# One dependence graph for two instruction streams, list-scheduled per engine, in place of weaving two in-order lists

## Chip, cores, metric

One Trainium2 chip, eight cores, each with its own four sequences (data parallel; no traffic between cores). The metric is the device time in microseconds of the slowest core. Cores 0 to 3 are one die, 4 to 7 the other. In many executions of every kernel here (the one before showed clocks of 0.793 to 0.932 in the seven runs beside e1, five of them slow) the cores of one or both dies run at a lower granted TensorE clock; such a run is called slow, and is not compared with a fast one.

## The reference, cut to what matters

```python
# x (32, 2048, 1024) float32; two layers, each with three sub-layers; RMS norm after the last
for l in range(2):
    h = modulate(rms_norm(x, norm_ffn1[l]), sh1, sc1)
    x = x + 0.5 * g1 * swiglu(h, ffn1_w_gu[l], ffn1_w_down[l])        # d_ff 2816
    h = modulate(rms_norm(x, norm_mix[l]), sh2, sc2)
    x = x + g2 * token_mix(h, ...)   # one input projection; mixer A: dense attention, 6 heads;
                                     # B: windowed attention, 6 heads; C: latent attention, 4 heads;
                                     # gates, one output projection
    h = modulate(rms_norm(x, norm_ffn2[l]), sh3, sc3)
    x = x + 0.5 * g3 * swiglu(h, ffn2_w_gu[l], ffn2_w_down[l])
return rms_norm(x, final_norm)
```

## The kernel before

The whole program is written out as straight-line instructions, in tiles of 512 tokens. The builder first records two lists of operations. Stream F has the norms, feed-forward layers and projections, stream M the attention, gates and output projection. M of one sequence runs beside F of another. Each stream has its own buffers; in PSUM, F has two banks and M six. In the profiles fb is a bank of F, sb and ob are banks of M (scores and outputs above all), hF is F's normalised input, tmpf and nr are its scratch, q, kA, kB and kC are queries and keys by mixer, pT is the probabilities, mt is M's scratch; wF and wM are weights. QK is the product of queries and keys, PV that of probabilities and values. `weave` then merges the lists by a model of the chip, and the merged order becomes each engine's queue. Semaphore waits follow from recorded reads and writes.

```python
LAT = 0.1; MODE_SWITCH = 0.12; DMA_LAT = 2.0
DMA_RATE = 200e3        # bytes per us, one server for all queues
SLACK = 0.5

def weave(streams):
    # o.v = phase + share of the phase's TensorE work that lies before the operation
    ...
    while True:
        cands = []
        for i, st in enumerate(streams):
            if heads[i] >= len(st.ops):
                continue
            o = st.ops[heads[i]]                 # only the head of each stream
            if any(n not in toks for n in o.need):
                continue
            cands.append((est(o), i, o))         # modelled start
        ...
        mn = min(c[0] for c in cands)
        best = min((c for c in cands if c[0] <= mn + SLACK), key=lambda c: (c[2].v, c[0]))
        st = streams[best[1]]
        while True:                              # run the head, and what is glued to it
            o = st.ops[heads[best[1]]]; heads[best[1]] += 1
            run(o)                               # advances the engine, reads, writes; appends to order
            if not o.glue: break
    return order, max(et.values()), busy
```

The norm (F's statistics are eight matmuls with a matrix of ones):

```python
def rsqrt_rows(st, bk, br, nr, inv_n):           # all on VectorE, each depends on the one before
    ts(st, ms, bk[0:nr, :], inv_n, EPS, ALU.mult, ALU.add, [br], [nr_r[0]])
    ts(st, y.bitcast(I32), ms.bitcast(I32), -0.5, MAGIC, ALU.mult, ALU.add, [nr_r[0]], [nr_r[1]], fast=True)
    for _ in range(2):
        stt(st, t, y, -0.5, y, ALU.mult, ALU.mult, [nr_r[1]], [nr_r[2]])
        tt_(st, "dve", t, t, ms, ALU.mult, [nr_r[2], nr_r[0]], [nr_r[2]])
        stt(st, y, t, 1.5, y, ALU.add, ALU.mult, [nr_r[2], nr_r[1]], [nr_r[1]])

def norm(l, m, s):
    norm_stats()
    for c in range(KC):
        t, tr = tmp()
        tt_(F, "dve", t[:], xc(c), nr_y[:], ALU.mult, [xF_r[c], nr_r[1]], [tr])
        act(F, hc(c), t[:], AF.Identity, [tr, mods_r[l][m]], [hF_r[c]], scale=mA(l, m, s, c), bias=mB(l, m, s, c))
```

The softmax here doesn't subtract the row's maximum and nothing guards it: scores larger than these inputs give would overflow.

## Time and profile before

| | before |
|---|---|
| median of the first 3 runs (lowest to highest) | 17,184 us (16,484 to 17,991) |
| span of the profiled fast run, core 7 (core 0) | 16,515.5 (16,465.9) us |
| TensorE busy, core 7 | 14,310 us, 87% |
| mean granted clock, core 7 (core 0) | 0.929 (0.931) |
| core 0: TensorE idle / at half clock / of that, busy | 2,179 / 2,260 / 1,319 us |

Two of these three runs are slow ones, so the median says little; 16,484 is fast. The last row is from the trace's clock record and the matmuls in it. "Busy" counts matmuls at whatever clock they ran: on core 0 one of 512 columns follows another after 216 ns at full clock and after 427 ns at half (medians of start to start in this trace). A span therefore has three parts: idle time, half of the busy time that lay in half clock (lost to the clock), and the rest, which is the work at full clock and whatever else the profile counts as busy (drains, the tail of a matmul before a gap: an estimate, from the 0.38 us that a lone matmul shows against 0.216 in a row).

### The profile page before, as it was taken

What the parts mean: (1) busy time and instruction counts of PE and PEld (TensorE: products, weight loads), DVE (VectorE), ACT (ScalarE), POOL (GpSimd) and SP (SyncE); (2) the same over time, 40 slices, a digit from 0 to 9 for tenths busy, and PEclk for the clock granted to TensorE, in tenths of its full rate; (3) what the DMA queues carried; (4) which work ended last, traced back from release to release, by engine and by line L of the source; (5) the groups of instructions that cost most, each with busy time, mean ns of one, the idle gap of its engine ahead of it and who ended that gap; (6) DMA issues with size and microseconds to landing.
All of it is one profiled execution on the core that took longest, in us unless ns stands there. A gap on an engine that the chain in (4) does not pass through costs nothing.

```text
span 16515.5 us, 199324 instructions; the slowest of 8 cores (16449.4 to 16515.5 us)
## 1 busy us (share of the span) xinstructions
PE 14310.3 (87%) x63128; PEld 5831.8 (35%) x63128; DVE 6429.4 (39%) x8558; ACT 5883.1 (36%) x7980; POOL 1591.9 (10%) x1365
## 2 busy tenths in 40 slices
PE   7878887888898898899888998898898889888888
PEld 2323333333333333333333333333333333333333
DVE  2334333433434334434434434434433444434333
ACT  1123443332332433434414343234433333434421
POOL 0001111110001100101100010000001110010000
PEclk8989998999999999999999999999999999999988
DMA  8555435654446343545544444444445443344344
GB/s 215 166 178 148 130 112 155 147 151 143 130 151 174 126 128 119 158 134 164 143 149 142 134 156 136 146 123 128 135 137 153 139 140 117 125 145 132 107 135 133
DMA packets 949560, 2346.30 MB, mean 142 GB/s; under 512 B 221478, under 2 KB 332972, under 8 KB 940364
## 3 DMA queue, kind: packets, MB, share of 16 engines
q1 hardware_dynamic: 918604, 2235.36, 42.9%
q0 software_dynamic: 29952, 98.19, 3.9%
q8 instruction: 553, 9.06, 0.2%
q14 instruction: 451, 3.69, 0.1%
HBM read 2056.36 MB, written 375.00 MB: 147 GB/s over the span
## 4 chain that ended last, share of the span: by engine, by line
PE 74%; DVE 9%; issue 6%; ACT 6%; DMA 3%; POOL 1%; SPq 1%; DVEq 0%; ACTq 0%; POOLq 0%
PE fb L510 53%; PE sb L510 12%; PE ob L510 9%; ACT pT L519 3%; DVE nr L526 2%; DVE pT L522 1%; DVE tmpf L522 1%; ACT hF L519 1%; DVE mt L1121 1%; DVE nr L522 1%; ACT mt L519 1%; DVE nr L533 1%; DMA mt<-xs 1%; SPq L543 1%; POOL tmpf L522 1%
## 5 line engine op out<-in xcount | busy, mean ns | idle before, releaser
L510 PE MATMUL fb<-hF,wF 128*128 128x512 bf16 x25600 | 6927.5, 393 | 799.2 <-ACT hF L519 428.0
L510 PEld LDWEIGHTS fb<-hF,wF 128*128 128x128 bf16 x25600 | 2478.2, 100 | 4395.3 <-issue 1877.2
L510 PE MATMUL fb<-actb,wF 128*128 128x512 bf16 x11520 | 3042.3, 383 | 50.2 <-DMA wF<-wts 17.3
L519 ACT ACTIVATE pT<-sb 128x1024 bf16<-128x1024 f32 x2560 | 2514.8, 1024 | 1293.3 <-PE sb L510 1278.9
L510 PE MATMUL ob<-pT,vv 128*128 128x512 bf16 x6176 | 1855.0, 372 | 468.0 <-DVE pT L522 211.2
L519 ACT ACTIVATE tmpf<-fb 128x512 f32<-128x512 f32 (+1 forms) x1409 | 842.8, 598 | 3421.2 <-PE fb L510 3407.9
L526 DVE SCALAR_TENSOR_TENSOR tmpf<-tmpf,fb 128x512 f32<-128x512 f32 x1408 | 965.8, 686 | 2727.2 <-ACT tmpf L519 2598.0
L510 PEld LDWEIGHTS fb<-actb,wF 128*128 128x128 bf16 x11520 | 1117.7, 98 | 1485.1 <-issue 210.1
L522 DVE TENSOR_TENSOR actb<-tmpf,fb 128x512 bf16<-128x512 f32 x1536 | 1056.1, 688 | 1258.8 <-PE fb L510 1034.9
L510 PE MATMUL sb<-hM,wM 128*128 128x512 bf16 x4160 | 1297.1, 388 | 30.1 <-DMA wM<-wts_bf 30.1
L526 DVE SCALAR_TENSOR_TENSOR xF<-fb,modG,xF 128x512 f32<-128x512 f32 x512 | 384.4, 751 | 2339.9 <-PE fb L510 2338.6
L519 ACT ACTIVATE hF<-xF 128x512 bf16<-128x512 f32 x896 | 532.9, 627 | 1996.3 <-DVE xF L526 1493.0
L519 ACT ACTIVATE mt<-sb 128x512 f32<-128x512 f32 (+2 forms) x808 | 595.0, 737 | 1387.1 <-PE sb L510 1123.0
L522 POOL TENSOR_TENSOR o<-mt 128x512 bf16<-128x512 f32 x256 | 369.9, 1445 | 7385.7 <-DVE mt L1121 6686.3
L510 PEld LDWEIGHTS ob<-pT,vv 128*128 128x128 bf16 x6176 | 553.2, 99 | 1292.4 <-issue 834.5
L1121 DVE RECIPROCAL mt<-mt 128x512 f32<-128x512 f32 x256 | 857.9, 3351 | 46.2 <-ACT mt L519 34.6
L519 ACT ACTIVATE hF<-tmpf,mods,modA 128x512 bf16<-128x512 f32 x768 | 558.0, 805 | 871.8 <-DVE tmpf L522 871.6
L510 PE MATMUL sb<-q,kA 64*128 64x512 bf16 x3072 | 559.7, 394 | 330.3 <-ACT pT L519 175.2
L519 ACT ACTIVATE mt<-ob 64x512 f32<-64x512 f32 (+1 forms) x760 | 451.4, 594 | 698.0 <-PE ob L510 588.4
L510 PE MATMUL sb<-q,kC 96*128 96x512 bf16 x2048 | 698.7, 381 | 0.4 <-ACT pT L519 0.3
L522 POOL TENSOR_TENSOR mt<-mt 128x512 f32<-128x512 f32 x256 | 324.4, 1267 | 3658.3 <-DVE mt L526 3409.5
L540 DVE COPY mt<-ob 64x512 f32<-64x512 f32 x512 | 351.7, 687 | 821.7 <-PE ob L510 751.5
(77 smaller groups left out, 8862.1 us busy)
## 6 DMA issues: line engine op xcount, KB each, us to landing
wF<-wts_bf SPq DMA_DIRECT2D x1530, 512.0 KB, 3.8
wF<-wts_bf SPq DMA_DIRECT2D x960, 352.0 KB, 3.2
wM<-wts_bf SPq DMA_DIRECT2D x600, 512.0 KB, 4.3
wF<-adaw SPq DMA_DIRECT2D x144, 512.0 KB, 5.2
xs<-xF SPq DMA_DIRECT2D x128, 512.0 KB, 3.5
mt<-xs SPq DMA_DIRECT2D x256, 256.0 KB, 6.1
xs<-mt SPq DMA_DIRECT2D x256, 256.0 KB, 3.1
xF<-xs SPq DMA_DIRECT2D x128, 512.0 KB, 7.5
```

The costliest lines, as they stand in the source:

```text
L510: st.op("pe", lambda E: E.matmul(out, lhsT=lhsT, rhs=rhs, start=start, stop=stop, skip_group_check=True), reads=reads, writes=writes, cost ...
L519: st.op("act", lambda E: E.activation(out=out, in_=in_, func=func, **kw), reads=reads, writes=writes, cost=c_act(n))
L522: st.op(eng, lambda E: E.tensor_tensor(out=out, in0=a, in1=b, op=op), reads=reads, writes=writes, cost=c_dve(n) if eng == "dve" else c_poo ...
L526: st.op("dve", lambda E: E.scalar_tensor_tensor(out=out, in0=a, scalar=scalar, in1=b, op0=op0, op1=op1), reads=reads, writes=writes, cost= ...
L533: f = lambda E: E.tensor_scalar(out=out, in0=a, scalar1=s1, scalar2=s2, op0=op0, op1=op1)
L540: st.op("dve", lambda E: E.tensor_copy(out=out, in_=in_), reads=reads, writes=writes, cost=c_dve(n))
L543: st.op(eng, lambda E: E.dma_start(out=out, in_=in_), reads=reads, writes=writes, chan=chan, nbytes=nbytes, need=need, give=give)
L1121: M.op("dve", lambda E: E.reciprocal(out=den, in_=den), reads=[denr], writes=[denr], cost=c_rec(TT))
```

## The change

The intent is that an operation should not have to stand behind earlier operations of its own stream with which it shares neither data nor engine. The core of the diff:

```diff
-DMA_RATE = 200e3
-SLACK = 0.5
+DMA_RATE = 350e3
+CAST_SLOWER = 2.0
+SLACK = 0.25
+def dependences(streams):
+    ...                                   # o.ins: each predecessor through a read, write or queue
 def weave(streams):
-    heads = [0] * len(streams)
-    ...                                   # the loop shown above
+    dependences(streams)
+    fut = {e: [] for e in engs}           # per engine: known ready time, by time
+    av = {e: [] for e in engs}            # per engine: ready now, by o.v
+    while len(order) < n:
+        best = None
+        for e in engs:                    # the engine that can start something first
+            if av[e]: t = et[e]
+            elif fut[e]: t = max(et[e], fut[e][0][0])
+            else: continue
+            if best is None or t < best[0]: best = (t, e)
+        t, e = best
+        f, a = fut[e], av[e]
+        while f and f[0][0] <= t + SLACK:
+            r, q, o = heapq.heappop(f)
+            heapq.heappush(a, (o.v, q, o))
+        v, q, o = heapq.heappop(a)        # of those ready within SLACK, the oldest by phase
+        t = max(t, o.ready)
+        ...                               # advance the engine, release the successors
```

Cuts: glued operations become one unit with several instructions; the tokens `need` and `give` (a whole tile stored before another stream may load it) are replaced by reads and writes of each piece in DRAM; loads that cast from float32 count double in the model. No instruction, buffer or bank rotation changes.

## The prediction

> **What bounds the kernel now.** I read the page first, then the waits of TensorE, the windows by stage, and the timeline around single stalls. The page says that TensorE is the bound, not at its peak, and not at its full clock:
>
> ```profile
> PE 14310.3 (87%) x63128; PEld 5831.8 (35%) x63128; DVE 6429.4 (39%) x8558; ACT 5883.1 (36%) x7980; POOL 1591.9 (10%) x1365
> ...
> PEclk8989998999999999999999999999999999999988
> ...
> PE 74%; DVE 9%; issue 6%; ACT 6%; DMA 3%; POOL 1%; SPq 1%; DVEq 0%; ACTq 0%; POOLq 0%
> ```
>
> No other engine is busy for even 40% of the span, the DMA engines move 142 GB/s, and the chain that ended last lies on TensorE for 74%. The other 26% of it are hops through VectorE and ScalarE.
>
> The windows by stage (busy time by engine, granted clock, DMA share) show three stages. Up to 1,280 us and from 15,880 us on only the F stream (feed-forward layers, norms, projections) has work; between them F and the M stream (attention, gates) run together:
>
> ```profile
> 0.00:1280.00 1280.00, 1018.80 (x3799) 351.06 (x3800) 368.23 (x599) 270.42 (x406) 86.39 (x102) 0.90 0.64 180
> 1280.00:15880.00 14600.00, 12781.14 (x57155) 5272.12 (x57153) 5832.69 (x7623) 5498.41 (x7391) 1505.46 (x1263) 0.93 0.46 139
> 15880.00:16515.00 635.00, 510.36 (x2176) 208.59 (x2176) 228.51 (x336) 114.28 (x184) 0.00 (x0) 0.88 0.41 133
> ```
>
> The middle stage holds 1,819 of the 2,205 us in which TensorE is idle, though there two independent streams could cover for each other. The waits of TensorE in it say where (us in total, times, longest):
>
> ```profile
> PE fb L510 <- ACT hF L519: 443.9, 129, 24.7
> PE ob L510 <- DVE pT L522: 211.2, 101, 5.6
> PE sb L510 <- ACT pT L519: 158.4, 332, 10.1
> PE fb L510 <- DVE tmpf L522: 148.9, 64, 9.7
> ...
> PE sb L510 <- DVE mt L526: 119.9, 28, 24.2
> PE ob L510 <- DVE mt L540: 100.5, 119, 3.5
> ```
>
> The first and fourth are the norms: the first matmuls after a norm wait for hF. The others are attention: PV waits for the probabilities, QK for the exponential that frees its bank. One stall from the timeline (start, length, what, idle before it):
>
> ```profile
> 5954.03 0.69 DVE L533 TENSOR_SCALAR nr<-fb 128x512 f32<-128x512 f32 x1
> ...
> 5960.15 4.91 DVE L522 TENSOR_TENSOR tmpf<-xF,nr 128x512 f32<-128x512 f32 x8
> 5960.94 5.77 ACT L519 ACTIVATE hF<-tmpf,mods,modA 128x512 bf16<-128x512 f32 x8 [8.53 <-DVE tmpf L522]
> ...
> 5961.90 4.12 PE L510 MATMUL fb<-hF,wF 128*128 128x512 bf16 x6 [9.21 <-ACT hF L519]
> ```
>
> From the statistics to the first normalised chunk lie eight dependent VectorE operations, a multiply and an activation, some 8 us, and TensorE has nothing of M in its queue to do meanwhile. The clock pays too:
>
> ```profile
> 5940.00:5952.00 12.00, 11.17 (x56) 4.62 (x54) 4.02 (x6) 7.16 (x9) 0.00 (x0) 1.00 0.40 136
> 5952.69:5961.90 9.21, 0.01 (x2) 0.04 (x1) 8.23 (x13) 0.96 (x2) 0.00 (x0) 0.68 0.00 0
> 5961.90:5975.00 13.10, 9.71 (x37) 3.07 (x37) 11.49 (x14) 9.61 (x13) 1.78 (x1) 0.70 0.11 40
> ```
>
> The clock is 1.00 before the stall, and 0.68 and 0.70 in it and after it. In the trace's clock record core 7 spends 2,277 us at one half and 157 us at 0.8125.
>
> **The ledger of the span.** A dense stretch of F, 176 matmuls in 38.16 us, gives 216 ns for one 512-column matmul. 57,600 such slots (two 64-row matmuls that run side by side count as one) make 12,442 us, the fp32 ones 248, the narrower ones 284, and the 1,056 groups of 64-row matmuls add about 190 ns each at their borders (312 ns start to start instead of 216 in the trace), 200 us. So the work takes **13,170 us** at full clock and the span is 3,345 us above it. Of these 2,205 are idle. About 1,300 us of TensorE's work lies in half-clock time and so costs 650 too much. The remaining 490 fit the drain after each of 2,746 gaps, some 0.17 us, which the profile counts as busy (a lone matmul shows 0.38 us).
>
> [...]half-clock stretches are multiples of 3.41 us, and of the windows that come just before one, three in four are busy for at most a third. [...]Here 0.8125 appears for 157 us on core 7 and never on cores 0 to 3[...].[...]
>
> **The change, part by part.** Instruction counts stay the same on every engine (62,839 matmuls, 8,558 VectorE, 7,978 ScalarE in both programs), and so do buffers and bank rotation. So the 13,170 us stay. What changes is the order: before, an operation could only be placed after all earlier ones of its own stream, whatever their engine; now only real dependences and queues count. The modelled DMA rate goes from 200 to 350 GB/s and the slack from 0.5 to 0.25 us. I read both orders on TensorE.
>
> Part 1, norms. There are 95 of them in the overlap. The M matmuls between a norm's statistics and F's next matmul had a median of 8 before; now it is some 24. As work at 216 ns the median is 2.4 us before and 3.9 now, the lowest quarter 1.0 and 2.6. Summed over the norms, what lacks to an 8.3 us chain falls from 501 to 370 us, a factor of 0.74. In the trace these stretches were idle for 786 us, and the first eight matmuls after them for 85. So about 225 us are saved.
>
> Part 2, attention. TensorE work between two successive QK groups of mixer A must cover two exponentials of 1.02 us. It was below 1.1 us in 52% of the cases and is in 15% now; the summed lack to 2.0 us falls from 471 to 185. QK and PV waits for exponentials are 223 us; times 0.6 that saves 130. The waits of PV for VectorE (211 and 100 us) and of the next tile's QK for it (120) I expect to shrink by a third, 140 us; the order around mixer B itself hardly moved.
>
> Part 3, rope and broadcasts, DMA and the F-only stages. About 170 us of waits for the head norms' broadcasts lose perhaps 50. F alone keeps its single buffers (PSUM pair, hF, xF), so I give its two stages 30.
>
> Part 4, what follows from fewer stalls. Idle falls by about 575; with a third fewer gaps the drains lose 150. With a median of 3.9 us of work in an 8 us chain, many norms rise above the third of a window that goes with a drop. If the half-clock work in the overlap (1,119 us, 560 lost) halves, that saves 280.
>
> The sum is 225 + 130 + 140 + 50 + 30 + 150 + 280 = 1,005 us. Against it I put 200 us for new stalls (below). From about 16,500 us that leaves **15,700 us**, 4.8% less. Both figures are for fast runs; the median of before, 17,184, is a slow run.
>
> **Rivals.** First, **the static order does not fit the chip**. The greedy order packs consumers closer to their modelled ready times, and the 350 GB/s of the model stands against 139 measured in the overlap. [...]For it: the first QK of five of the seven later attention phases comes 2 to 11 us of work after the last projection, where 85 or so lay before for most. Against it: DMA ends only some 70 us of TensorE's waits in the overlap now, with weight slots several steps deep. It would eat half the gain: 16,050 to 16,300, or with a bad order no gain at all.
>
> [...]
>
> Third, **nearly all overlap stalls vanish**, because the queues of VectorE, ScalarE and SyncE improve as well, which I have not counted. Idle below 900 and half clock below 800 us would give 14,900 to 15,100.
>
> **Range and chances.** The central working gives 15,700; the first rival sets the upper end at 16,300, half of the third the lower at 15,100. Faster by over 2% means under 16,170: 0.85. Within 2%: 0.12. Slower: 0.03, as nothing is added.
>
> **What would show it.** Right: TensorE's busy time down by some 400 us (drains, half clock) with the same counts; the waits of fb on ACT hF and of sb on ACT pT down by a third and over half; the mean clock up from 0.93 to about 0.95; the F-only stages unchanged; VectorE and ScalarE as busy as before. Wrong: DMA waits of several hundred us, a clock at or below 0.93 in spite of less idle time[...], or waits of the norms as long as before with M matmuls beside them that themselves wait.

## The result

| | before | after |
|---|---|---|
| median of 4 runs (lowest to highest) | 16,834 us (16,476 to 17,991) | 15,380 us (15,199 to 16,175) |
| fast runs over fast runs | 1 | 0.9221 (95%: 0.9194 to 0.9248) |
| core 0: span | 16,466 | 15,198 |
| core 0: TensorE idle | 2,179 | 1,303 |
| core 0: at half clock / of that, busy | 2,260 / 1,319 | 1,073 / 651 |

The ratio is the mean time of one kernel's fast runs over that of the other's of the same rounds, so it is not quite the ratio of the medians. The change is 7.8% faster; the output is correct.

The page after (core 0 was the slowest):

```profile
PE 13894.7 (91%) x63128; PEld 5726.4 (38%) x63128; DVE 6398.2 (42%) x8558; ACT 5860.8 (39%) x7980; POOL 1588.8 (10%) x1365
...
PEclk9999999999999999999999999999999999999998
...
PE 79%; DVE 10%; issue 4%; DMA 4%; ACT 2%; POOL 1%; SPq 1%; DVEq 0%; ACTq 0%; POOLq 0%
```

The counts are those of before, VectorE and ScalarE are as busy in microseconds as before, and TensorE is busy for 416 us less with the same matmuls (core 7 before, core 0 after; 392 with core 0 in both). In the ledger of the prediction that can only be clock and drains, the drains being its estimate. The windows by stage (busy time and count by engine; clock, DMA share, GB/s):

```profile
0.00:1280.00 1280.00, 1040.75 (x3982) 359.32 (x3983) 381.45 (x617) 297.60 (x438) 88.98 (x106) 0.93 0.68 186
1280.00:14565.00 13285.00, 12352.47 (x56971) 5158.61 (x56971) 5782.42 (x7598) 5449.16 (x7359) 1499.84 (x1259) 0.97 0.50 152
14565.00:15198.00 633.00, 501.46 (x2176) 208.51 (x2176) 234.34 (x345) 114.04 (x184) 0.00 (x0) 0.89 0.40 136
```

The last stage, F alone, is what it was. The gain is in the overlap, where 932 us are idle instead of 1,819 and the clock is 0.97 instead of 0.93. The waits of TensorE in that stage (us in total, times, longest):

```profile
PE fb L562 <- ACT hF L571: 200.4, 78, 7.6
PE ob L562 <- DVE pT L574: 176.8, 100, 4.8
PE fb L562 <- DVE tmpf L574: 106.5, 66, 12.9
PE ob L562 <- ACT pT L571: 79.8, 187, 2.0
PE fb L562 <- DVE actb L574: 57.3, 119, 3.2
PE sb L562 <- DVE mt L578: 37.7, 6, 12.1
...
PE sb L562 <- ACT pT L571: 16.5, 33, 2.3
...
PE ob L562 <- DVE mt L592: 13.1, 25, 3.9
```

(L562, L571, L574, L578 are the helper lines that were L510, L519, L522, L526.) The norms, hF and tmpf, fall from 593 to 307 us; QK's wait for the exponential from 158 to 17; the waits for copies out of ob from 100 to 13. The wait of PV for mixer B's probabilities (pT on VectorE) hardly moves, 211 to 177.

The same norm in both traces, one that falls into M's gates and output projection. Before, the stretch from its statistics to F's next matmul and the 12 us behind it:

```profile
6159.97:6167.97 8.00, 1.52 (x8) 0.49 (x5) 7.03 (x11) 1.52 (x3) 0.00 (x0) 0.76 0.05 22
...
6168.00:6180.00 12.00, 11.12 (x37) 3.81 (x38) 5.00 (x9) 8.35 (x13) 2.52 (x2) 0.73 0.92 239
```

and after:

```profile
5663.50:5671.70 8.20, 6.51 (x31) 2.76 (x29) 7.21 (x12) 1.76 (x3) 0.00 (x0) 1.00 0.93 302
5671.70:5684.00 12.30, 11.49 (x48) 4.22 (x49) 5.50 (x9) 9.30 (x16) 4.78 (x4) 1.00 0.95 293
```

The chain is as long (8.0 and 8.2 us) and VectorE as busy in it. TensorE has 1.5 us of work in it before and 6.5 after. Behind it, before, the clock is 0.73 and in 12 us 37 matmuls are done; after, it stays at 1.00 and 48 are done. The timeline names the work that was put there:

```profile
5665.31 3.19 PE L562 MATMUL sb<-mg,wM 128*128 128x512 bf16 x14
5668.33 1.67 PE L562 MATMUL ob<-mg,wM 128*128 128x512 bf16 x7
5671.71 1.58 PE L562 MATMUL fb<-hF,wF 128*128 128x512 bf16 x5 [1.71 <-DVE tmpf L574]
```

They are output projections (mg with w_out), which in the kernel before came from 6,176 us on, after the start of F's next step. Not every norm is covered. The stall that the prediction showed still stands (7.50 us of idle before F's next matmul, 9.21 before). It falls into mixer B, which has little TensorE work:

```profile
5464.60:5475.50 10.90, 2.42 (x22) 0.93 (x21) 9.36 (x15) 2.76 (x4) 0.00 (x0) 0.77 0.06 19
```

On core 0 the 1,268 us divide as follows: idle time 876 less (2,179 to 1,303), loss to half clock 334 less (1,319/2 to 651/2), and the rest of the busy time 58 less.

### The profile page after: what moved, and what is told of

The parts are those of the page before. It is cut to its first block, busy times and chain, and to the rows that moved or that the text cites.

```text
span 15197.9 us, 199367 instructions; the slowest of 8 cores (15164.9 to 15197.9 us)
## 1 busy us (share of the span) xinstructions
PE 13894.7 (91%) x63128; PEld 5726.4 (38%) x63128; DVE 6398.2 (42%) x8558; ACT 5860.8 (39%) x7980; POOL 1588.8 (10%) x1365
## 4 chain that ended last, share of the span: by engine, by line
PE 79%; DVE 10%; issue 4%; DMA 4%; ACT 2%; POOL 1%; SPq 1%; DVEq 0%; ACTq 0%; POOLq 0%
PE fb L562 55%; PE sb L562 13%; PE ob L562 11%; DVE nr L578 2%; DVE pT L574 2%; DVE tmpf L574 1%; DVE nr L574 1%; DVE nr L585 1%; DVE mt L1164 1%; ACT pT L571 1%; ACT hF L571 1%; DMA out<-xF 1%; SPq L595 0%; DVE actb L574 0%; DMA wts_bf<-wF 0%
## 5 line engine op out<-in xcount | busy, mean ns | idle before, releaser
L562 PE MATMUL fb<-hF,wF 128*128 128x512 bf16 x25600 | 7031.6, 386 | 436.2 <-ACT hF L571 203.7
L562 PEld LDWEIGHTS fb<-hF,wF 128*128 128x128 bf16 x25600 | 2433.2, 99 | 3830.9 <-issue 1281.3
L562 PE MATMUL fb<-actb,wF 128*128 128x512 bf16 x11520 | 3336.6, 381 | 63.6 <-DVE actb L574 24.6
L571 ACT ACTIVATE pT<-sb 128x1024 bf16<-128x1024 f32 x2560 | 2540.5, 1021 | 1743.4 <-PE sb L562 1710.8
L562 PE MATMUL ob<-pT,vv 128*128 128x512 bf16 x6176 | 2029.1, 368 | 308.2 <-DVE pT L574 176.8
L578 DVE SCALAR_TENSOR_TENSOR tmpf<-tmpf,fb 128x512 f32<-128x512 f32 x1408 | 965.0, 685 | 2717.8 <-ACT tmpf L571 2438.9
L571 ACT ACTIVATE tmpf<-fb 128x512 f32<-128x512 f32 (+1 forms) x1409 | 840.8, 597 | 2863.1 <-PE fb L562 2856.0
L562 PEld LDWEIGHTS fb<-actb,wF 128*128 128x128 bf16 x11520 | 1117.0, 98 | 1481.3 <-issue 182.3
L574 DVE TENSOR_TENSOR actb<-tmpf,fb 128x512 bf16<-128x512 f32 x1536 | 1052.2, 685 | 1071.6 <-PE fb L562 982.7
L562 PE MATMUL sb<-hM,wM 128*128 128x512 bf16 x4160 | 1388.0, 380 | 7.8 <-DMA wM<-wts_bf 6.8
L578 DVE SCALAR_TENSOR_TENSOR xF<-fb,modG,xF 128x512 f32<-128x512 f32 x512 | 384.2, 750 | 2203.8 <-PE fb L562 2201.8
L571 ACT ACTIVATE hF<-xF 128x512 bf16<-128x512 f32 x896 | 533.9, 625 | 1657.9 <-DVE xF L578 1374.2
L571 ACT ACTIVATE mt<-sb 128x512 f32<-128x512 f32 (+2 forms) x808 | 588.8, 735 | 1253.1 <-PE sb L562 887.6
L574 POOL TENSOR_TENSOR o<-mt 128x512 bf16<-128x512 f32 x256 | 367.7, 1436 | 6480.2 <-DVE mt L1164 5977.0
L562 PEld LDWEIGHTS ob<-pT,vv 128*128 128x128 bf16 x6176 | 554.5, 98 | 1155.6 <-issue 683.7
L571 ACT ACTIVATE hF<-tmpf,mods,modA 128x512 bf16<-128x512 f32 x768 | 552.9, 801 | 712.4 <-DVE tmpf L574 712.3
L562 PE MATMUL sb<-q,kC 96*128 96x512 bf16 x2048 | 752.2, 381 | 3.0 <-ACT pT L571 2.9
L574 POOL TENSOR_TENSOR mt<-mt 128x512 f32<-128x512 f32 x256 | 324.6, 1268 | 3632.2 <-DVE mt L578 3535.6
L562 PE MATMUL ob<-hM,wM 128*128 128x512 bf16 x1984 | 681.8, 382 | 5.4 <-DMA wM<-wts_bf 3.4
L571 ACT ACTIVATE mt<-ob 64x512 f32<-64x512 f32 (+1 forms) x760 | 450.2, 592 | 556.0 <-PE ob L562 492.9
L562 PEld LDWEIGHTS sb<-hM,wM 128*128 128x128 bf16 x4160 | 405.8, 98 | 487.4 <-issue 20.1
```

Source lines behind the costliest of these rows:

```text
L562: st.op("pe", lambda E: E.matmul(out, lhsT=lhsT, rhs=rhs, start=start, stop=stop, skip_group_check=True), reads=reads, writes=writes, cost ...
L571: st.op("act", lambda E: E.activation(out=out, in_=in_, func=func, **kw), reads=reads, writes=writes, cost=c_act(n))
L574: st.op(eng, lambda E: E.tensor_tensor(out=out, in0=a, in1=b, op=op), reads=reads, writes=writes, cost=c_dve(n) if eng == "dve" else c_poo ...
L578: st.op("dve", lambda E: E.scalar_tensor_tensor(out=out, in0=a, scalar=scalar, in1=b, op0=op0, op1=op1), reads=reads, writes=writes, cost= ...
```

## The experiments

**How they are read.** The four chips of the experiments were slow far more often than the first (88 of 103 runs, against 4 of the 8 timed ones there). The rounds still give clean numbers, because often one die alone is disturbed and the cores do not talk to each other. The kernel before took 16,450 to 16,470 us (median of a die's four cores) at a clock of 0.931 to 0.933 on a die without disturbance, on every one of the chips. So each kernel below is given by its undisturbed dies: the fastest die medians, which come back with the same clock on at least two dies where not said otherwise. Ratios are over 16,460. In the kept profiles a disturbed die is one whose cores spend time at a granted clock of 0.8125: 12,446 to 12,577 us on die 0 of the last kernel of the table against 391 to 519 on its die 1, 1,542 to 1,571 us on die 1 of the kernel with fillers against 0 on its die 0. The time at half clock hardly differs between the two dies (788 to 816 and 837 to 885 us; 679 to 718 and 727 to 745). So what makes a die slow here is the clock of 0.8125, not more half clock. All kernels gave correct results.

| kernel | undisturbed die, us | clock | ratio |
|---|---|---|---|
| before | 16,450 to 16,470 | 0.931 to 0.933 | 1 |
| before, new constants | 16,302 to 16,317 | 0.931 to 0.933 | 0.991 |
| before, short norm | 16,235 to 16,239 | 0.937 to 0.938 | 0.986 |
| after, program order on each engine | 15,858 to 15,860 | 0.937 to 0.939 | 0.963 |
| after, old constants | 15,701 to 15,712 | 0.950 | 0.954 |
| after, old DMA rate only | 15,554 to 15,571 | 0.956 to 0.957 | 0.945 |
| after, program order on TensorE only | 15,511 to 15,517 | 0.949 to 0.950 | 0.943 |
| after, old slack only | at most 15,508 (one die, once) | 0.952 | at most 0.942 |
| after, fillers | 15,245 to 15,263 | 0.976 | 0.927 |
| after, DMA rate 600 GB/s | 15,196 to 15,216 | 0.960 to 0.963 | 0.924 |
| **after** | 15,173 to 15,189 | 0.964 to 0.966 | 0.922 |
| after, short norm | 14,994 to 15,030 | 0.967 to 0.970 | 0.912 |
| after, short norm, no slack | 14,857 to 14,879 | 0.969 to 0.971 | 0.903 |

The theory was that the graph lets work of the other stream into TensorE's stalls, and that idle time and half clock both fall for that reason. The first rival to test: the change also moved three constants of the model.

### Which part of the change

```diff
 # e1_old_constants, on the kernel after
-DMA_RATE = 350e3; CAST_SLOWER = 2.0; SLACK = 0.25
+DMA_RATE = 200e3; CAST_SLOWER = 1.0; SLACK = 0.5
```

> The kernel after, with the three constants of the scheduler's model put back to those of before (DMA rate 200 GB/s, slack 0.5 us, no extra cost for the casting loads). Theory, the dependence graph does it: the order on TensorE keeps most of its new shape (lack of work behind norms 411 us, after 370, before 501; QK gaps under 1.1 us of work 20%, after 15%, before 52%), so 15,250 to 15,500 us in fast runs, ratio 0.925 to 0.94. Rival, the constants do it: 16,000 us or more, ratio at least 0.97.

Measured 15,701 to 15,712: between theory and rival. The graph alone is worth 755 us, not the 960 to 1,200 that I expected, and the constants on top of it 525.

```diff
 # e2_before_new_constants, on the kernel before
-DMA_RATE = 200e3; SLACK = 0.5
+DMA_RATE = 350e3; SLACK = 0.25      # and casting loads at twice their bytes in the model
```

> The kernel before, its in-order weaving kept, with the three new constants (350 GB/s, 0.25 us, casting loads at twice their cost). Theory, the graph does it: the lack of work behind norms stays (498 us against 501), QK gaps under 1.1 us fall from 52 to 37%, so only 100 to 350 us are gained: 16,100 to 16,400 us, ratio 0.98 to 0.995. Rival, the constants do it: 15,700 us or less, ratio at most 0.955.

Measured 16,302 to 16,317 on undisturbed dies, as the theory said. By themselves the constants give 150 us. So 755 and 150 are separate, and some 375 us come only when both are there.

```diff
 # e3_program_order_on_each_engine, on the kernel after, in dependences()
+            if o.eng in ("pe", "act", "dve", "pool", "sp"):
+                p = last.get(o.eng)          # the stream's last operation on this engine
+                if p is not None:
+                    pre.setdefault(p, -1.0)  # may not start before it
+                last[o.eng] = o
```

> The kernel after, but on every engine each stream's operations keep their program order; only the engines of one stream are let loose from each other. Theory A, it is the decoupling of the engines that gains: 15,200 to 15,450 us, ratio 0.92 to 0.94. Theory B, it is reordering within an engine (a load, an exponential or a copy that passes an earlier one of its own stream): 15,900 us or more, ratio 0.965 or more. The order on TensorE says A for attention (QK gaps 14.5% as after) and B for norms (lack 473 against 370), so the middle, some 15,450, would mean both.

Measured 15,858 to 15,860, just short of theory B (fast runs alone: 0.967, 0.939 to 0.994, a verdict of unclear at 2%). The middle of 15,450, expected from TensorE's order, was too good by 400. Waits of the undisturbed core 4 over its whole span show why:

```profile
PE fb L568 <- ACT hF L577: 516.0, 202, 20.9
...
PE sb L568 <- DMA q<-qs: 111.8, 8, 27.5
```

The norms wait nearly as before (593 us on core 0 of the kernel before over the whole span, 319 after). There is also a wait of 112 us for q, which does not occur after: with each stream's DMA issues in program order the small loads of q stand behind others in SyncE's queue. Around one such wait (8,303 to 8,328 us) SyncE issues the loads of keys and values (kC, kB, vv) from 8,295 to 8,323 us, and only then those of q.

```diff
 # e4_program_order_on_tensore: the same with
+            if o.eng in ("pe",):
```

> The kernel after, with program order per stream on TensorE alone; all other engines and queues free. If it matters that matmuls pass earlier matmuls of their own stream, 15,400 us or more (ratio 0.935 or more; the lack behind norms rises from 370 to 424 us). If TensorE gains only through the other engines' queues and through mixing two streams, 15,150 to 15,280 us, ratio about 0.92 to 0.925.

Measured 15,511 to 15,517, as the first of the two said, so matmuls that pass matmuls of their own stream are worth 333 us. In the order after these are about 3,000 of 60,000, about half of them M's gates and PVs, then F's and the output projections, and none moves by more than 39 places.

Put in a row, these steps lead from before to after: new constants 16,460 to 16,310; engines of a stream let loose from each other, 15,859; free order on all but TensorE, 15,514; free order on TensorE too, 15,181. That is 150, 451, 345 and 333 us. In another succession the shares would differ, as e1 shows. And the 451 us are not the decoupling of engines alone: e3 keeps the finer DRAM dependences (a piece in place of a whole tile) and the new rule for which operation is placed next. No run separates these three.

### Which constant, and a control

> The kernel after, unchanged, as a control beside the next three on one chip: 15,180 us on a die that keeps its clock (0.965), as on the chip of its first runs, where such a die took 15,165 to 15,198. If this chip is slower by itself, the undisturbed dies of the kernel before (16,456 there) will tell.

Measured 15,173 to 15,187 on undisturbed dies, as on the first chip.

```diff
 # e5_old_dma_rate_only, on the kernel after      # e8_dma_rate_600
-DMA_RATE = 350e3                                 # -DMA_RATE = 350e3
+DMA_RATE = 200e3                                 # +DMA_RATE = 600e3
```

> The kernel after with one constant put back: the modelled DMA rate at 200 GB/s. With all three put back an undisturbed die took about 15,700 us, 520 more than after. Theory, the DMA rate is the one that counts, since the model's loads then come late and its TensorE order waits for data that the chip has long had: 15,600 to 15,800 us on an undisturbed die. Rival, the slack or the casting loads do it: under 15,350.

> The kernel after with the modelled DMA rate at 600 GB/s, four times what the trace shows. If what counts is only that the model never holds matmuls back for data, this is as good as 350: 15,100 to 15,250 us on an undisturbed die. If the model's rate has to be near the truth (152 GB/s here), TensorE now waits on DMA for hundreds of us: 15,400 or more.

The old rate took 15,554 to 15,571, just below the range of the theory: it costs 380 us. The fast rate took 15,196 to 15,216: it costs 25 us or so (0.2%), a part of it clock, since the higher of these dies spent 200 to 239 us at 0.8125 in its profile. The trace shows 154 GB/s on average, so the best of the three values tried is not the one closest to the mean rate. Of these, the low rate is dear and the high one is not. The third constant, the double cost of casting loads, was not tried alone. That a low rate orders TensorE's work after loads that have long landed is my reading; no run shows it by itself.

```diff
 # e7_old_slack_only, on the kernel after
-SLACK = 0.25
+SLACK = 0.5
```

> The kernel after with the slack alone at its old 0.5 us. Putting back all three constants costs 520 us and the DMA rate alone 375. If the slack carries the rest: 15,280 to 15,350 us on an undisturbed die. Its order on TensorE speaks against that (lack behind QK groups 166 us against 185, behind norms 375 against 370): then 15,100 to 15,230.

This chip was slow in all four runs. The least disturbed die took 15,508 us at 0.952. The profile of a slow run has some 1,400 us at half clock, and these alone would give a clock of 1 - 0.5 x 1,400/15,508 = 0.955, so that die was hardly disturbed. I estimate the cost of the old slack at 250 to 330 us; it is not measured cleanly. With the 380 of the rate that is more than the 525 of all three constants together, so these costs don't add up either. My expectation, no cost, was drawn from the lack of work behind norms and QK groups in TensorE's order, and that was a bad gauge: this order has less lack than the one after (166 and 375 us against 185 and 370) and is slower. In e3 it had failed too.

### The clock

```diff
 # e6_fillers, on the kernel after, where the order is written out (in short, not the code itself)
+if o is the first matmul of an accumulation and the model leaves TensorE idle over 1 us before it:
+    for _ in range(int((o.start - bank_free) * 0.75 / 0.2165)):
+        P.op("pe", matmul(bank, lhsT=RA, rhs=cbf[:, 0:512], start=True, stop=True), [const_r], [bank_r])
```

> The kernel after with 1,781 matmuls without use, put into three quarters of each gap that the scheduler's own model leaves on TensorE before the first matmul of an accumulation (into the bank that this matmul then clears; results stay right). They do no work, and shorten no chain. Theory, each idle window costs twice, once as idle and once as a half clock after it: half-clock time falls from 1,073 to 500 us or less, the mean clock rises to 0.98 or more, and 100 to 200 us are gained: 14,980 to 15,100 us on an undisturbed die. Rival, the clock follows something else, or the fillers get into the way of work: clock at 0.965 and 15,200 us or more.

The clock did rise, to 0.976, short of the 0.98 expected. The windows by stage of its undisturbed core 0:

```profile
0.00:1162.00 1162.00, 1011.51 (x4023) 373.74 (x4025) 336.25 (x554) 202.53 (x332) 84.05 (x102) 0.96 0.68 187
1162.00:14630.00 13468.00, 12668.17 (x58376) 5265.73 (x58373) 5825.22 (x7652) 5544.44 (x7464) 1505.44 (x1263) 0.98 0.49 152
14630.00:15271.00 641.00, 575.88 (x2514) 239.10 (x2511) 239.14 (x353) 114.15 (x184) 0.00 (x0) 0.95 0.40 134
```

The record of the kernel before shows what goes ahead of a drop. On its core 0, 223 of the 224 half-clock stretches are one or more times 3.41 us long. Of the full-clock stretches, cut into windows of 3.41 us, all 183 windows that were less than 40% busy were the last before a drop, 25 of 40 at 40 to 50%, and 1 of 3,871 at 60% or more. With gaps filled the clock rises from 0.965 to 0.976, so a part of the half clock here did come from idle windows. Yet the kernel lost 70 us where 100 to 200 of gain were expected. Half-clock time fell from 1,073 to 745 us, not to 500, but of the 328 us only 108 were busy ones, and those are worth 54. The fillers took 426 us. Idle time fell by 288, so the other 130 or so took the place of work. The half clock that could be bought off in this way was mostly half clock of an idle engine (220 of the 328 us), which costs nothing. In the last stage the clock goes from 0.89 to 0.95 and the stage takes as long as before.

### What still bounds it

```diff
 # e9_after_short_norm on the kernel after, e10_before_short_norm on the kernel before
-MAGIC = 1597463007.0
+MAGIC = 1595932665.0
-        for _ in range(2):
-            stt(st, t, y, -0.5, y, ...)
+        for _ in range(1):
+            stt(st, t, y, -0.703952253, y, ...)
-            stt(st, y, t, 1.5, y, ...)
+            stt(st, y, t, 1.6819141, y, ...)
```

> The kernel after with one step of the inverse square root's iteration in place of two (other constants, error 0.00065 of the value, below a bf16 step): three VectorE operations, some 2.3 us, out of each chain of 8.3 us from a norm's statistics to its first matmul. Theory, the norms' chains set most of what TensorE still waits for (about 580 of 1,274 us idle lie in them): 110 chains give back some 160 us of idle and 50 of half clock, 14,930 to 15,060 us on an undisturbed die. Rival, the list scheduler already hides them or another wait takes their place: 15,120 us or more.

> The kernel before with the same shorter chain. There 940 us of idle lie in the norms, so the same cut is worth more than in the kernel after if that change's gain came in good part from covering norms: 250 to 400 us, 16,060 to 16,210 us on an undisturbed die (from 16,460). If the order, and not the length of the chains, decides: 16,350 or more.

After: 14,994 to 15,030, about 170 us less, as expected; the norms' chains still set waits that nothing covers. Before: 16,235 to 16,239, 222 less, below the expected 250. The same cut is worth more before than after, so covering norms is part of the change's gain, but by a factor of 1.3 only. My reading, which no run shows by itself: the chain costs the most where nothing stands beside it, and such norms are left in both kernels, in F alone at both ends and in mixer B.

```diff
 # e13_short_norm_no_slack, on e9
-SLACK = 0.25
+SLACK = 0.0
```

> The kernel after with the short norm chain (15,010 us on an undisturbed die) and the slack at 0 in place of 0.25 us: each engine takes the operation that is ready first, and an older one may not make it wait. A slack of 0.5 took at most 15,508 us on the least disturbed die, some 300 more than 0.25. Theory, slack is idle time that the scheduler chooses to make: no slack gains again, 14,750 to 14,950 us on an undisturbed die. Rival, 0.25 is a middle between idle time and the order of the phases: 15,000 us or more.

Measured 14,857 to 14,879 on undisturbed dies, as the theory said, and one run fast on both (14,870 us beside 16,483 of the kernel before in the same rounds). That is the best, about 9.7% under before. It also shows what a disturbed die looks like, in the cores of its profiled run:

```profile
die 0 (median of its cores): 16670.8 us, clock 0.835
die 1 (median of its cores): 14910.3 us, clock 0.966
```

One program, one launch, and 1,760 us between two dies.

## Why the prediction was right, and where its sizes were off

The time (15,700 against 15,380 as the median, 15,180 to 15,200 fast) lay in the range, on its fast side; the gain was 7.8% where 4.8% was worked out. The central figure was some 520 us too high: 200 of them were the reserve for new stalls, 263 lay in the parts (1,268 measured, 1,005 summed), where sizes too small outweighed one too large. The wide range, and not the sum, covered this.

- **The work stays, the stalls shrink.** Right: the counts are the same, the busy time apart from the loss to half clock changes by 58 us only, and the gain is mostly idle time and clock in the overlap. A line was misread on the way: of the 26% of the chain that lie off TensorE, VectorE and ScalarE are 15; issue is 6 and DMA 3.
- **Norms: mis-sized.** The step was "what lacks to an 8.3 us chain falls from 501 to 370 us, a factor of 0.74", applied to 786 us. On core 0 the idle time in these stretches fell from some 746 to 405 us, and in the eight matmuls behind from 82 to 21, so 402 us against 225. After, the idle time is near the lack; before, it was 245 above. So the M work inside the stretch must itself have waited, and the new order cured that as well, which counting matmuls in TensorE's queue alone cannot show. The third rival named this (the other queues), and e3 against e4 puts a size on it for all stalls together: 345 us for order within the other engines' queues.
- **Attention.** Waits for exponentials fell from 223 to 96 us, 127 against 130 predicted. The waits of PV and QK for VectorE fell by 203 (431 to 228) against 140. Mixer B hardly moved, as said.
- **Rope and broadcasts** fell by some 95 (168 to 73 us) against 50. **F alone** gave more than the 30 at the start: the first M matmul comes at 1,129 instead of 1,202 us on core 0. But F has run 120 matmuls fewer by then (3,432 against 3,552, some 26 us of work), so a part of this is an earlier start of M and not a faster F. The end stayed.
- **Drains: mis-sized the other way.** 58 us against 150. Gaps of at least 0.1 us fell from 2,474 to 1,517, but the rest of the busy time did not follow at 0.17 us each. At 58 us for 957 gaps, 0.06 us each, drains would be some 165 of the 490 us that the ledger put down to them (an estimate); what the rest is, no run shows.
- **Half clock.** 334 us against 280; the clock is 0.965, not 0.95.
- **The first rival did not come.** I held back 200 us for new stalls. Waits for DMA in the overlap fell from 69 to 38 us although the first QK of a phase comes sooner. The sign was even wrong for the rate: e5 shows that the lower modelled rate is what costs.
- **A clock of 0.8125** was granted for no time in the fast run (0 us on all cores). In a slow run of the same program cores 0 and 4 spent 7,201 and 9,730 us at it:

```profile
die 0 (median of its cores): 16203.6 us, clock 0.884
die 1 (median of its cores): 16540.9 us, clock 0.858
```

That takes back what the change gained, but it hits the kernel before in the same way (18,015 us in the same rounds), and which runs it hits is not explained by any run here.

What stays open: why the slack costs so much, and the exact cost of 0.5; what the casting loads' constant does alone; and how the constants and the graph come to give 375 us only together.

## What to carry to other kernels

Where two independent streams share engines, letting every queue have its own order paid here: in the succession tested, a third of the gain came from decoupling a stream's engines (with the finer dependences), a quarter each from free order on the other queues and on TensorE. Judge such an order by the trace and not by counting one queue, and try the scheduler's constants on the chip: too careful a model of the DMA cost 380 us, too bold a one 25 or so. Here an idle TensorE cost twice only where work followed at half clock (651 of the 1,073 us at half clock on core 0 after were busy), and matmuls without use did not pay (70 us lost): fill the gaps with real work or leave them.
